# Moving the start addresses of the operands of fp32r products within 256 bytes

## The chip, the cores and the metric

The kernel runs on one core of a Trainium2 chip. The metric is the device time of one execution in microseconds (us), the median of several runs. Before the change it is 2085.33 us (2084.98 to 2087.54, three runs).

## The reference

Two layers (DEPTH 2) over 512 tokens of 1024 features, all in float32. Each layer computes, from a normalised and modulated `h`:

```python
proj = h @ w_in[l]
qa, ka, va, cq, ckv, kr, z, xbc, dt_raw, gates = jnp.split(proj, _IN_OFFSETS, axis=-1)
...  # differential attention oa (4 heads), latent attention ob (8 heads), SSD scan ys (16 heads)
merged = ga * (ya @ w_branch_a[l]) + gb * (yb @ w_branch_b[l]) + gc * (ys @ w_branch_c[l])
x = x + g_m * (merged @ w_out[l])
h = _rmsnorm(x, norm_ffn[l]) * (1 + sc_f) + sh_f
u = _causal_dwconv(h @ ffn_w_up[l], ffn_conv_w[l], ffn_conv_b[l])
ua, uv = jnp.split(u, 2, axis=-1)
x = x + g_f * ((jax.nn.silu(ua) * uv) @ ffn_w_down[l])
```

## The kernel before, in words

Nearly all of TensorE's work is products with model weights. A float32 product is made of three fp32r products: both operands are split into a high part and a rest (`wh`, `wl` for weights, `hh`, `hl` for the normalised activations; `yh`, `yl` for the branch outputs, `mh`, `ml` for the merged ones and `gh`, `gl` for the gated ones), and high times high, high times rest and rest times high are summed in PSUM. `load` (L114) brings 512 KB of weights by DMA from SP's queue into a tile `wr`; `split` (L126) makes `wh` with one ScalarE activation (L132) and `wl` with one VectorE subtraction (L133). Three buffers of each stand in the pool `wp`; they are used in the order 0, 2, 1, 0, 2, 1.

Four forms of product use them:

- `feat_groups` with `mm3` (L140 to L143): the weights are the stationary operand (128 x 128), the activations move, 512 columns at a time. The moving operands are `hh`/`hl`, `yh`/`yl`, `mh`/`ml`, `gh`/`gl`.
- `feat_halves` (L231), around the seams between stages: as before, in two halves of 256 columns. Some of its weights stand in another pool (`wo` beside the out product, `wd` beside the down product) so that they can wait there.
- `tok_groups` (L192, matmuls L220 to L222): the activations `hh`/`hl` are stationary and the weights move, 256 columns at a time. It makes `z` and the queries, keys and values of the differential attention.
- `latent_product` (L269, matmuls L295 to L297): as `tok_groups`, with 432 columns.

While one matmul streams its moving operand, the weights of the next matmul are loaded. A statement about two addresses below is therefore about the moving operand of one matmul and the stationary operand of the next.

The order of TensorE's instructions is written out by hand in the attention stages and at the seams (`manual_schedule`); there the weight products fill the time between the steps of the attention heads. Elsewhere the scheduler of the tile framework orders them. VectorE also sums the modulation vectors (`macc`, L518) in the gaps.

SBUF tiles lie one after another in the order of the pools, 32 bytes the least step. From the tile shapes: the constants (`cst`) begin at byte 16512 of a partition and end at 22720. There `big` begins: `x16` at 22720, `hh` at 39104, `hl` at 55488. `wp` follows at 71872: three `wr`, three `wh` (the first at 84160), three `wl` (96448) of 4096 bytes each, two `wg` of 2048. The small tiles `sm` lie from 112832 to 119936. Above them the stage pools: `gh` begins at 122752, `yh` at 130944, `mh` at 163712. From the top down lie pools of the right side: the first buffer of `wo` begins at 197600, of `wd` at 178112.

Below, the residue of a tile is its start modulo 256, and d is the moving operand's start less the stationary operand's, modulo 256. Tiles are addressed within themselves in steps of 512 bytes or more (except the second 432-column block of a latent tile), so that d is the same along a product. Before the change:

| product | moving | stationary | d |
|---|---|---|---|
| 512 columns, h | 192 | 192 | 0 |
| 512 columns, y, m, g | 128 | 192 | 192 |
| 256 columns, `tok_groups` | 192 (weights) | 192 (h) | 0 |
| 256-column halves of m and g, weights in `wp` or `wd` | 128 | 192 | 192 |
| 256-column halves of m, weights in `wo` | 128 | 224 | 160 |
| 256-column halves of h | 192 | 192 | 0 |
| 432 columns, seven of eight weight groups | 192 (weights) | 192 (h) | 0 |
| 432 columns, last weight group of layer 0 | 128 (weights) | 192 (h) | 192 |

Of the kernel before, what the change touches and what calls it, by code (L numbers as in the profile page):

```python
# [9 lines left out]
F32 = mybir.dt.float32  # L10
F32R = mybir.dt.float32r
I32 = mybir.dt.int32
AF = mybir.ActivationFunctionType
ALU = mybir.AluOpType
# [4 lines left out]
P = 128  # L19
S = 512  # L20
# [45 lines left out]
def trunk_kernel(ctx: ExitStack, tc: tile.TileContext, a: dict, out: bass.AP):  # L66
# [23 lines left out]
    def small(shape, name, bufs=4):  # L90
        return sm.tile(shape, F32, name=name, tag=name, bufs=bufs)
# [5 lines left out]
    nc.vector.memset(ones, 1.0)  # L97
    tri = cst.tile([P, P], F32, name="tri")
    nc.gpsimd.affine_select(tri, ones, pattern=[[1, P]], compare_op=ALU.is_ge, fill=0.0, base=0, channel_multiplier=-1)
    nhalf = cst.tile([P, 1], F32, name="nhalf")  # L100
    nc.vector.memset(nhalf, -0.5)

    sel = cst.tile([P, SSM_H], F32R, name="sel")
    nc.vector.tensor_copy(out=sel, in_=ident[:, 0:SSM_H])
    nc.vector.tensor_copy(out=sel[32:48], in_=ident[0:SSM_H, 0:SSM_H])
    def rstd_of(ss, n, width, name):
        ms = small([P, n], name + "_ms")
        nc.vector.tensor_scalar(out=ms, in0=ss, scalar1=1.0 / width, scalar2=EPS, op0=ALU.mult, op1=ALU.add)
        r = small([P, n], name + "_r")
        nc.gpsimd.tensor_tensor(out=r, in0=ms, in1=nhalf.broadcast_to([P, n]), op=ALU.pow)  # L110
        return r


# [9 lines left out]
            nc.sync.dma_start(out=dst, in_=src)  # L123
        return raw

    def split(raw, n, scales=None, pool=None):  # L126
        hi = (pool or wp).tile([P, 1024], F32R, name="wh")
        lo = (pool or wp).tile([P, 1024], F32R, name="wl")
        for o, m, col in scales or ((0, n, None),):
            sl = slice(o, o + m)  # L130
            if col is None:
                nc.scalar.activation(hi[:, sl], raw[:, sl], AF.Copy)  # L132
                nc.vector.tensor_tensor(out=lo[:, sl], in0=raw[:, sl], in1=hi[:, sl], op=ALU.subtract)  # L133
            else:
                nc.scalar.activation(hi[:, sl], raw[:, sl], AF.Copy, scale=col)
                nc.vector.scalar_tensor_tensor(out=lo[:, sl], in0=raw[:, sl], scalar=col, in1=hi[:, sl],
                                               op0=ALU.mult, op1=ALU.subtract)
        return hi, lo

    def mm3(o, lh, ll, rh, rl, first, last):  # L140
# [51 lines left out]
    def tok_groups(w, segs, hh, hl, evac):  # L192

        width = sum(n for _, n in segs)

        st = {}

        def group(half):
            def prep():
                rows = w[half * 512:(half + 1) * 512, :].rearrange("(k p) c -> p k c", p=P)  # L200
                raw = wp.tile([P, 1024], F32, name="wr", bufs=3)
                rv_, off = raw[:, 0:4 * width].rearrange("p (k c) -> p k c", k=4), 0
                for c, n in segs:
                    nc.sync.dma_start(out=rv_[:, :, off:off + n], in_=rows[:, :, c:c + n])
                    off += n
                return split(raw, 4 * width)

            def mm(weights):
                wh, wl = weights
                if half == 0:  # L210
                    st["banks"] = [mbank().rearrange("p (t c) -> p t c", t=2) for _ in range(2)]
                for t in range(T):
                    bank = st["banks"][t // 2]
                    o = bank[:, t % 2, 0:width]
                    ts_ = slice(t * P, (t + 1) * P)
                    first, last = half == 0 and t % 2 == 0, half == 1 and t % 2 == 1
                    for k in range(4):
                        kk = 4 * half + k
                        sl = slice(k * width, (k + 1) * width)
                        nc.tensor.matmul(o, hh[:, kk, ts_], wh[:, sl], start=first and k == 0, stop=False)  # L220
                        nc.tensor.matmul(o, hh[:, kk, ts_], wl[:, sl], start=False, stop=False)  # L221
                        nc.tensor.matmul(o, hl[:, kk, ts_], wh[:, sl], start=False, stop=last and k == 3)  # L222
                    if last:
                        evac(t // 2, bank)
                    yield 1.28
            return prep, mm
        return [group(0), group(1)]
# [3 lines left out]
    def feat_halves(w, cols, nk, rhs, evac, joint, pool=None, spare=0):  # L231


        st = {}

        def prep():
            out = []
            for k0 in range(0, nk, 4):
                n = min(4, nk - k0)
                raw = load([(0, (n, 256), w[k0 * P:(k0 + n) * P, cols[0]:cols[0] + 256].rearrange("(k p) c -> p k c", p=P))])  # L240
                out.append([x[:, 0:n * 256].rearrange("p (k i c) -> p i k c", k=n, i=2) for x in split(raw, n * 256, None, pool if nk - k0 <= 4 * spare else None)])
            return out

        def mm(weights, h):
            if h == 0 or not joint:
                st["banks"] = [mbank(), mbank()]
            for k in range(nk):
                vh, vl = weights[k // 4]
                xh, xl = rhs(k)
                for i in range(2):  # L250
                    o = st["banks"][i][:, HALF[h]]
                    mm3(o, vh[:, i, k % 4], vl[:, i, k % 4], xh[:, HALF[h]], xl[:, HALF[h]], k == 0, k == nk - 1)
                if k == nk - 1 and not (joint and h == 0):
                    for i in range(2):
                        if joint:
                            evac(i, st["banks"][i])
                        else:
                            evac(i, st["banks"][i][:, HALF[h]], HALF[h])
                yield 0.64
        return prep, mm  # L260
# [8 lines left out]
    def latent_product(l, pool, hh, hl):  # L269
# [4 lines left out]
        def group(g):  # L274
            rows = a["w_in"][l][g * 256:(g + 1) * 256, :].rearrange("(k p) c -> p k c", p=P)
            raw = wp.tile([P, 1024], F32, name="wr", bufs=3)
            rv_ = raw[:, 0:2 * width].rearrange("p (k c) -> p k c", k=2)
            nc.sync.dma_start(out=rv_[:, :, 0:416], in_=rows[:, :, C_CQ:C_CQ + 416])
            nc.sync.dma_start(out=rv_[:, :, 416:width], in_=rows[:, :, C_DT:C_DT + 16])
            return split(raw, 2 * width, None, pool if g == 3 else None)  # L280

        def prep():
            return [group(g) for g in range(3)]
# [94 lines left out]
    def vectors(l, vp):  # L378
# [5 lines left out]
            nc.sync.dma_start(out=t[r:r + n, :], in_=src)  # L384
        rv = rowv[l]
        for nm, key in (("dtb", "ssm_dt_bias"), ("alog", "ssm_a_log"), ("dvec", "ssm_d")):
            t_ = cst.tile([P, SSM_H], F32, name=f"{nm}{l}")
            nc.sync.dma_start(out=t_, in_=a[key][l:l + 1, :].broadcast_to([P, SSM_H]))
            rv[nm] = t_
        rows(r2, 0, a["ssm_conv_b"][l].rearrange("(r p) -> r p", p=P), 16)  # L390
# [30 lines left out]
        lsum = vp.tile([P, 2], F32, name="lsum")  # L421
        nc.vector.tensor_reduce(out=lsum, in_=pr, axis=AX.X, op=ALU.add)
        nc.scalar.activation(lsum, lsum, AF.Exp)
        lam = cst.tile([P, 1], F32, name=f"lam{l}")
        nc.vector.scalar_tensor_tensor(out=lam, in0=lsum[:, 0:1], scalar=0.8 - 0.6 * math.exp(-0.3 * l),
                                       in1=lsum[:, 1:2], op0=ALU.add, op1=ALU.subtract)
        rv["lam"] = lam
        for nm, key in (("q", "mla_q_norm"), ("k", "mla_k_norm")):
            w32 = cst.tile([P, ROPE], F32, name=f"w32{nm}{l}")
            nc.sync.dma_start(out=w32, in_=a[key][l:l + 1, NOPE:MLA_QK].broadcast_to([P, ROPE]))  # L430
            rv["w" + nm] = w32

# [61 lines left out]
    def mod_steps(l, j, pool=None):  # L494
# [27 lines left out]
        def total():  # L522
            mp = mbank()
            for q in range(4):
                ins = nc.tensor.transpose(out=mp[:, q * P:(q + 1) * P], in_=acc[0][:, q * P:(q + 1) * P], identity=ident)
                if pool:
                    tc.keep_in_program_order(ins)
            cs_ = slice(4 * j, 4 * j + 4)
            tot = small([P, 4], "modsum")
            nc.vector.tensor_reduce(out=tot, in_=mp.rearrange("p (q r) -> p q r", q=4), axis=AX.X, op=ALU.add)  # L530
            nc.vector.tensor_tensor(out=mod[l][:, cs_], in0=tot, in1=vec[l][:, cs_], op=ALU.add)

# [171 lines left out]
    def norm_halves(np_, x, l, v_norm, sh0, sc0):  # L704

        s1 = norm_scale(l, v_norm, sc0)
        sacc = np_.tile([P, S], F32, name="sacc")
        hh, hl = h_tiles()
        st = {}

# [31 lines left out]
    def mix(l, x, hh, hl, ckr, cq, latp, scope):  # L742
# [123 lines left out]
        with ssd_scope:  # L866
            tails = []
            for g in range(SSM_G):
# [102 lines left out]
                                            in1=ecs[:, c, hd].unsqueeze(2).broadcast_to([P, 4, SSM_HD]), op=ALU.mult)  # L971
                    nc.vector.tensor_tensor(out=y[:, c], in0=y[:, c], in1=yo, op=ALU.add)
                nc.vector.scalar_tensor_tensor(out=y, in0=y, scalar=0.5, in1=sz, op0=ALU.mult, op1=ALU.mult)
                ss = small([P, T], "yss")
                for c in range(T):
                    jk = sp.tile([P, 256], F32, name="yo", bufs=2)
                    nc.scalar.activation(jk, y[:, c], AF.Square, accum_out=ss[:, c:c + 1])
# [23 lines left out]
        with ExitStack() as att:  # L1001
# [237 lines left out]
            def da_groups(h):  # L1239
                heads[h]["qk"] = qkn = dap.tile([P, T, 256], F32, name="qkn")  # L1240

                def qk_evac(tt, bank):
# [1 line left out]
                    nc.scalar.activation(raw, bank, AF.Copy)  # L1244
                    sq = dap.tile([P, 2, 256], F32, name="sq2", bufs=2)
                    nc.scalar.activation(sq, raw, AF.Square)
                    ss8 = small([P, 8], "dss8")
                    nc.vector.tensor_reduce(out=ss8, in_=sq.rearrange("p t (g d) -> p (t g) d", d=DA_D), axis=AX.X, op=ALU.add)
                    r8 = rstd_of(ss8, 8, 64.0, "dr8")
                    rg = raw.rearrange("p t (g d) -> p (t g) d", d=DA_D)  # L1250
# [30 lines left out]
            def da_unit(h, t):  # L1281
# [32 lines left out]
                def values():  # L1314
# [6 lines left out]
                    if t == T - 1:  # L1321
                        sq = dap.tile([P, T, P], F32, name="sq2", bufs=2)
                        pov = po.rearrange("p (t c) -> p t c", t=T)
                        nc.scalar.activation(sq, pov, AF.Square)
                        ss = small([P, T], "oss")
                        nc.vector.tensor_reduce(out=ss, in_=sq, axis=AX.X, op=ALU.add)
                        r_ = rstd_of(ss, T, 128.0, "on")
                        hd["on"] = dap.tile([P, T, P], F32, name="on", bufs=1)
# [252 lines left out]
```

## Time and profile before

| what | us |
|---|---|
| median of three runs | 2085.33 |
| the profiled execution, its own time | 2087.19 |
| its span, first to last instruction | 2085.2 |
| PE (TensorE matmuls) busy | 2060.7 |
| DVE (VectorE) busy | 1415.1 |
| ACT (ScalarE) busy | 923.4 |

The span is 2 us shorter than the execution's time; the rest lies before the first and after the last instruction. A matmul's record lasts longer than its share of the engine, since matmuls overlap: what one costs in a row of its kind is read from start to start in the timeline, and so done below.

### The profile page before, as it was taken

To read this page: it belongs to the slowest core of one execution; us is meant where nothing else is said; L and a number is where in the kernel's file an instruction comes from. 1 tells how busy PE (TensorE), PEld (TensorE's weight loads), DVE (VectorE), ACT (ScalarE), POOL (GpSimd) and SP (SyncE) were. 2 spreads that over 40 slices of the span, in tenths; PEclk is the share of its full clock that TensorE was granted. 3 is DMA by queue.
4 is the path that set the end of the run, shared out by engine and by line. 5 is a ranking of instruction groups with operands and counts; after the bars stand their busy time and mean duration, and the time that the engine had idled before them with its cause. 6 is when DMAs were issued, how large, how long until landed. Compare 5 with 4: busy or idle time off the path is not lost.

```text
span 2085.2 us, 30158 instructions
## 1 busy us (share of the span) xinstructions
PE 2060.7 (99%) x11469; PEld 1794.4 (86%) x11469; DVE 1415.1 (68%) x2731; ACT 923.4 (44%) x1702; POOL 136.0 (7%) x162
## 2 busy tenths in 40 slices
PE   8999999999999999999999999999999999999999
PEld 7889988899888988888898888889998888888888
DVE  7788887747876778657767887765566566553553
ACT  6744445535533444224344544454444334432431
POOL 4200011002100000000000000110020000000000
PEclk8999999999999999999999999999999999999999
DMA  8523232243455265655443222212333242323322
GB/s 268 154 61 92 71 117 86 86 123 105 143 157 171 85 189 171 193 175 159 156 136 91 71 61 88 64 48 79 95 89 93 91 132 91 101 91 96 97 91 81
DMA packets 224542, 237.20 MB, mean 114 GB/s; under 512 B 16126, under 2 KB 195742, under 8 KB 224142
## 3 DMA queue, kind: packets, MB, share of 16 engines
q1 hardware_dynamic: 221646, 232.63, 36.5%
q0 software_dynamic: 2752, 2.65, 0.5%
q8 instruction: 90, 1.47, 0.3%
q14 instruction: 54, 0.44, 0.1%
HBM read 226.30 MB, written 8.91 MB: 113 GB/s over the span
## 4 chain that ended last, share of the span: by engine, by line
PE 85%; DVE 5%; issue 5%; DMA 2%; POOL 1%; ACT 1%; SPq 0%; POOLq 0%; DVEq 0%; ACTq 0%
PE mb L141 20%; PE mb L142 20%; PE mb L143 20%; PE mb L220 3%; PE mb L222 3%; PE mb L221 3%; PE ab L1168 2%; PE mb L662 1%; PE ab L1136 1%; DMA wg<-in_ada_w_dram 1%; DVE wl L133 1%; PE ab L961 1%; DVE macc L518 1%; PE ab L1319 1%; PE ab L1078 1%
## 5 line engine op out<-in xcount | busy, mean ns | idle before, releaser
L141 PE MATMUL mb<-hh,wh 128*128 128x512 f32 (+1 forms) x1376 | 538.5, 392 | 2.9 <-DVE modsum L530 1.4
L143 PE MATMUL mb<-hh,wl 128*128 128x512 f32 (+1 forms) x1376 | 532.9, 387 | 0.0
L142 PE MATMUL mb<-hl,wh 128*128 128x512 f32 (+1 forms) x1376 | 532.5, 387 | 0.0
L133 DVE TENSOR_TENSOR wl<-wr,wh 128x1024 fp32r<-128x1024 f32 (+2 forms) x312 | 375.2, 1204 | 201.2 <-ACT wh L132 195.5
L132 ACT ACTIVATE wh<-wr 128x1024 fp32r<-128x1024 f32 (+2 forms) x312 | 324.5, 1041 | 337.3 <-PE mb L142 257.4
L141 PEld LDWEIGHTS mb<-hh,wh 128*128 128x128 f32 x1376 | 258.6, 188 | 53.4 <-DVE modsum L530 2.6
L143 PEld LDWEIGHTS mb<-hh,wl 128*128 128x128 f32 x1376 | 258.7, 188 | 51.4
L142 PEld LDWEIGHTS mb<-hl,wh 128*128 128x128 f32 x1376 | 259.0, 188 | 49.0 <-DVE hl L698 1.2
L1416 DVE SCALAR_TENSOR_TENSOR fu<-mb,vec,fu 128x510 f32<-128x510 f32 (+1 forms) x176 | 129.9, 746 | 91.2 <-ACT fu L1414 89.6
L220 PE MATMUL mb<-wh,hh 128*128 128x256 f32 x640 | 182.4, 285 | 0.0
L221 PE MATMUL mb<-wl,hh 128*128 128x256 f32 x640 | 181.2, 283 | 0.0
L222 PE MATMUL mb<-wh,hl 128*128 128x256 f32 x640 | 181.2, 283 | 0.0
L141 PE MATMUL mb<-gh,wh 128*128 128x512 f32 (+1 forms) x432 | 152.3, 353 | 0.0
L143 PE MATMUL mb<-gh,wl 128*128 128x512 f32 (+1 forms) x432 | 151.7, 351 | 0.0
L142 PE MATMUL mb<-gl,wh 128*128 128x512 f32 (+1 forms) x432 | 151.7, 351 | 0.0
L1414 ACT ACTIVATE fu<-mb,vec 128x512 f32<-128x512 f32 x88 | 67.7, 772 | 149.0 <-PE mb L143 149.0
L220 PEld LDWEIGHTS mb<-wh,hh 128*128 128x128 f32 x640 | 122.6, 192 | 0.8 <-ACT wh L132 0.4
L221 PEld LDWEIGHTS mb<-wl,hh 128*128 128x128 f32 x640 | 122.6, 192 | 0.4
L222 PEld LDWEIGHTS mb<-wh,hl 128*128 128x128 f32 x640 | 122.6, 192 | 0.0
L518 DVE SCALAR_TENSOR_TENSOR macc<-wg,c_act,macc 128x512 f32<-128x512 f32 x140 | 104.8, 749 | 22.9 <-DMA wg<-in_ada_w_dram 22.3
L141 PE MATMUL mb<-yh,wh 128*128 128x512 f32 x256 | 105.4, 412 | 0.9 <-ACT g L765 0.9
L142 PE MATMUL mb<-yl,wh 128*128 128x512 f32 x256 | 101.2, 395 | 0.0
(334 smaller groups left out, 3427.4 us busy)
## 6 DMA issues: line engine op xcount, KB each, us to landing
wr<-in_w_in_dram SPq DMA_DIRECT2D x88, 512.0 KB
wr<-in_ffn_w_up_dram SPq DMA_DIRECT2D x88, 512.0 KB
wg<-in_ada_w_dram SPq DMA_DIRECT2D x160, 256.0 KB
wr<-in_ffn_w_down_dram SPq DMA_DIRECT2D x40, 512.0 KB
wr<-in_w_in_dram SPq DMA_DIRECT2D x64, 256.0 KB
wm<-in_ada_w_dram SPq DMA_DIRECT2D x16, 512.0 KB
wr<-in_w_branch_c_dram SPq DMA_DIRECT2D x16, 512.0 KB
wr<-in_w_out_dram SPq DMA_DIRECT2D x16, 512.0 KB
```

Of the source, the lines that this page charges most:

```text
L132: nc.scalar.activation(hi[:, sl], raw[:, sl], AF.Copy)
L133: nc.vector.tensor_tensor(out=lo[:, sl], in0=raw[:, sl], in1=hi[:, sl], op=ALU.subtract)
L141: nc.tensor.matmul(o, lh, rh, start=first, stop=False)
L142: nc.tensor.matmul(o, lh, rl, start=False, stop=False)
L143: nc.tensor.matmul(o, ll, rh, start=False, stop=last)
L220: nc.tensor.matmul(o, hh[:, kk, ts_], wh[:, sl], start=first and k == 0, stop=False)
L221: nc.tensor.matmul(o, hh[:, kk, ts_], wl[:, sl], start=False, stop=False)
L222: nc.tensor.matmul(o, hl[:, kk, ts_], wh[:, sl], start=False, stop=last and k == 3)
L518: ins = nc.vector.scalar_tensor_tensor(out=acc[0], in0=rk, scalar=c_act[:, kk:kk + 1], in1=acc[0], op0=ALU.mult, op1=ALU.add)
L1168: nc.tensor.matmul(po[:, t * P:n], vv[:, j], st["pT"][:, j * P:(j + 1) * P], start=j == 0, stop=j == t)
L1414: nc.scalar.activation(u, bank, AF.Identity, bias=v[:, V_FCB + ti:V_FCB + ti + 1], scale=tap(2))
L1416: nc.vector.scalar_tensor_tensor(out=u[:, s_:], in0=bank[:, 0:S - s_], scalar=tap(2 - s_), in1=u[:, s_:], op0=ALU.mult, op1=ALU.add)
```

## The change

`split` loses its unused scaling argument and gains a shift. In `wp` the tiles `wh` and `wl` become 48 columns (192 bytes) longer, and each use starts at an offset of 0 to 3 times 64 bytes that undoes what the longer tiles add: every `wh` and `wl` then starts at one residue, 64 bytes higher where `shift=1` is passed (`tok_groups`, `feat_halves`, `latent_product`). In another pool the start is that of the tile plus `own`.

The first changed call below is the one in `tok_groups`, the second that in `latent_product`.

```diff
+    LINE = 16
+    uses = [0]
+    def split(raw, n, pool=None, shift=0, own=0):
+        if pool is None:
+            i = -uses[0] % 3
+            uses[0] += 1
+            at = ((i + shift) % 4, (i + 3 + shift) % 4)
+            hi, lo = [wp.tile([P, 1024 + 3 * LINE], F32R, name=nm)[:, LINE * o:LINE * o + n] for nm, o in zip(("wh", "wl"), at)]
+        else:
+            hi, lo = [pool.tile([P, 1024], F32R, name=nm)[:, own:own + n] for nm in ("wh", "wl")]
+        nc.scalar.activation(hi, raw[:, 0:n], AF.Copy)
+        nc.vector.tensor_tensor(out=lo, in0=raw[:, 0:n], in1=hi, op=ALU.subtract)
         return hi, lo
...
-                return split(raw, 4 * width)
+                return split(raw, 4 * width, shift=1)
...
-            return split(raw, 2 * width, None, pool if g == 3 else None)
+            return split(raw, 2 * width, pool if g == 3 else None, 1, 0 if l else LINE)
...
-    nhalf = cst.tile([P, 1], F32, name="nhalf")
+    nhalf = cst.tile([P, 9], F32, name="nhalf")
...
-        ms = small([P, n], name + "_ms")
+        ms = small([P, n], name + "_ms", 2)
...
-        r = small([P, n], name + "_r")
+        r = small([P, n], name + "_r", 3)
...
-            t_ = cst.tile([P, SSM_H], F32, name=f"{nm}{l}")
+            t_ = cst.tile([P, SSM_H], F32, name=nm)
...
-        sacc = np_.tile([P, S], F32, name="sacc")
+        sacc = np_.tile([P, S + 8 * (v_norm == V_NFFN)], F32, name="sacc")
```

The other edits set the sizes of what lies below: the row constants of the two layers (`dtb`, `alog`, `dvec`, `lam`, `w32q`, `w32k`) share one tile each, and small tiles have 2 or 3 buffers where they had 4 (also `modsum` 2, `yss`, `dss8` and `oss` 3). Worked out with these sizes, `cst` ends at 22720 - 480 + 32 = 22272 = 87 x 256, so `x16`, `hh`, `hl` and `wp` start at residue 0; `sm` starts at 113536 and is 832 bytes smaller, so the stage pools start at 119808 = 468 x 256, 128 bytes lower than before, and `yh`, `yl`, `mh`, `ml`, `gh`, `gl` have residue 0. `wo` moves from 224 to 192; `wd` stays at 192. After the change:

| product | moving | stationary | d |
|---|---|---|---|
| 512 columns, h, y, m, g | 0 | 0 | 0 |
| 256 columns, `tok_groups` | 64 (weights) | 0 (h) | 64 |
| 256-column halves of m, g, h, weights in `wp` | 0 | 64 | 192 |
| 256-column halves of m in `wo`, of g in `wd` | 0 | 192 | 64 |
| 432 columns, seven of eight weight groups | 64 (weights) | 0 (h) | 64 |
| 432 columns, last weight group of layer 1 | 192 (weights) | 0 (h) | 192 |

## Rows read from the trace of the kernel before

**Rows 1.** Parts 1 and 4 of the page: busy us by engine; shares of the last chain.

```profile
PE 2060.7 (99%) x11469; PEld 1794.4 (86%) x11469; DVE 1415.1 (68%) x2731; ACT 923.4 (44%) x1702; POOL 136.0 (7%) x162
...
PE 85%; DVE 5%; issue 5%; DMA 2%; POOL 1%; ACT 1%; SPq 0%; POOLq 0%; DVEq 0%; ACTq 0%
```

**Rows 2.** PE by form: line, output<-moving,stationary, shapes, count | busy us, mean ns | idle.

```profile
L141 PE MATMUL mb<-hh,wh 128*128 128x512 f32 x1312 | 520.2, 397 | 2.1 <-DVE modsum L530 1.4 <-DVE g L774 0.7
...
L220 PE MATMUL mb<-wh,hh 128*128 128x256 f32 x640 | 182.4, 285 | 0.0
...
L141 PE MATMUL mb<-gh,wh 128*128 128x512 f32 x272 | 107.6, 396 | 0.0
...
L141 PE MATMUL mb<-yh,wh 128*128 128x512 f32 x256 | 105.4, 412 | 0.9 <-ACT g L765 0.9
...
L1136 PE MATMUL ab<-ident,sb 128*128 128x128 f32 x240 | 42.1, 273 | 0.6 <-DVE mx L1151 0.5
...
L141 PE MATMUL mb<-mh,wh 128*128 128x256 f32 x128 | 36.0, 281 | 0.0
...
L141 PE MATMUL mb<-mh,wh 128*128 128x512 f32 x64 | 25.3, 395 | 0.0
...
L295 PE MATMUL mb<-wh,hh 128*128 128x432 f32 x64 | 23.1, 365 | 1.4 <-ACT wh L132 1.4
...
L141 PE MATMUL mb<-hh,wh 128*128 128x256 f32 x64 | 18.7, 292 | 0.8 <-ACT hh L697 0.8
...
L1467 PE MATMUL ab<-ident,x 128*128 128x128 f32 x32 | 4.2, 276 | 0.3 <-DVE x L1445 0.3
```

**Rows 3.** PE timeline (start us, duration us), h products, 178 starts, first and last.

```profile
1799.70 0.39 PE L143 MATMUL mb<-hh,wl 128*128 128x512 f32 x1
...
1839.83 0.39 PE L143 MATMUL mb<-hh,wl 128*128 128x512 f32 x1
```

**Rows 4.** PE timeline, down products of g, 173 starts, first and last.

```profile
1849.69 0.39 PE L141 MATMUL mb<-gh,wh 128*128 128x512 f32 x1
...
1889.83 0.39 PE L142 MATMUL mb<-gl,wh 128*128 128x512 f32 x1
```

**Rows 5.** PE timeline, token products, 86 starts, first and last.

```profile
245.80 0.28 PE L220 MATMUL mb<-wh,hh 128*128 128x256 f32 x1
...
255.99 0.28 PE L221 MATMUL mb<-wl,hh 128*128 128x256 f32 x1
```

**Rows 6.** PE timeline, halves of m: starts 1, 39 and 63 of one stretch.

```profile
1692.76 0.28 PE L142 MATMUL mb<-ml,wh 128*128 128x256 f32 x1
...
1697.07 0.28 PE L141 MATMUL mb<-mh,wh 128*128 128x256 f32 x1
...
1699.95 0.28 PE L141 MATMUL mb<-mh,wh 128*128 128x256 f32 x1
```

**Rows 7.** PE timeline, halves of g after a restart, 79 starts, first and last.

```profile
1072.80 0.28 PE L141 MATMUL mb<-gh,wh 128*128 128x256 f32 x1
...
1081.99 0.28 PE L141 MATMUL mb<-gh,wh 128*128 128x256 f32 x1
```

**Rows 8.** PE timeline, y products in an attention stage, 36 starts, first and last.

```profile
617.82 0.40 PE L142 MATMUL mb<-yl,wh 128*128 128x512 f32 x1
...
625.99 0.40 PE L141 MATMUL mb<-yh,wh 128*128 128x512 f32 x1
```

**Rows 9.** PE timeline, h products just after SSD matmuls, 37 starts, first and last.

```profile
188.69 0.39 PE L141 MATMUL mb<-hh,wh 128*128 128x512 f32 x1
...
196.89 0.39 PE L141 MATMUL mb<-hh,wh 128*128 128x512 f32 x1
```

**Rows 10.** Windows: stretch, busy us (count) of each engine, PEclk, DMA share, GB/s.

```profile
552.00:640.00 88.00, 86.36 (x425) 71.47 (x424) 67.53 (x128) 36.60 (x67) 5.60 (x6) 1.00 0.52 162
```

**Rows 11.** The last chain (start us, us): the head of the latent attention, layer 0.

```profile
293.20 1.02 POOL r_r L110
...
297.84 0.09 DVE r_ms L108
```

More of the change, by code (lines that the diff above doesn't have):

```diff
@@ L106, in rstd_of @@
     def rstd_of(ss, n, width, name):
-        ms = small([P, n], name + "_ms")
+        ms = small([P, n], name + "_ms", 2)
         nc.vector.tensor_scalar(out=ms, in0=ss, scalar1=1.0 / width, scalar2=EPS, op0=ALU.mult, op1=ALU.add)
-        r = small([P, n], name + "_r")
-        nc.gpsimd.tensor_tensor(out=r, in0=ms, in1=nhalf.broadcast_to([P, n]), op=ALU.pow)
+        r = small([P, n], name + "_r", 3)
+        nc.gpsimd.tensor_tensor(out=r, in0=ms, in1=nhalf[:, 0:1].broadcast_to([P, n]), op=ALU.pow)
         return r
@@ L124, in load @@
         return raw
[L126 to L137, printed above, removed]
+    LINE = 16
[10 more added lines that the diff above has]
+        nc.vector.tensor_tensor(out=lo, in0=raw[:, 0:n], in1=hi, op=ALU.subtract)
         return hi, lo
@@ L240, in prep @@
                 raw = load([(0, (n, 256), w[k0 * P:(k0 + n) * P, cols[0]:cols[0] + 256].rearrange("(k p) c -> p k c", p=P))])
-                out.append([x[:, 0:n * 256].rearrange("p (k i c) -> p i k c", k=n, i=2) for x in split(raw, n * 256, None, pool if nk - k0 <= 4 * spare else None)])
+                out.append([x[:, 0:n * 256].rearrange("p (k i c) -> p i k c", k=n, i=2) for x in split(raw, n * 256, pool if nk - k0 <= 4 * spare else None, 1)])
             return out
@@ L423, in vectors @@
         nc.scalar.activation(lsum, lsum, AF.Exp)
-        lam = cst.tile([P, 1], F32, name=f"lam{l}")
+        lam = cst.tile([P, 1], F32, name="lam")
         nc.vector.scalar_tensor_tensor(out=lam, in0=lsum[:, 0:1], scalar=0.8 - 0.6 * math.exp(-0.3 * l),
@@ L428, in vectors @@
         for nm, key in (("q", "mla_q_norm"), ("k", "mla_k_norm")):
-            w32 = cst.tile([P, ROPE], F32, name=f"w32{nm}{l}")
+            w32 = cst.tile([P, ROPE], F32, name=f"w32{nm}")
             nc.sync.dma_start(out=w32, in_=a[key][l:l + 1, NOPE:MLA_QK].broadcast_to([P, ROPE]))
@@ L528, in total @@
             cs_ = slice(4 * j, 4 * j + 4)
-            tot = small([P, 4], "modsum")
+            tot = small([P, 4], "modsum", 2)
             nc.vector.tensor_reduce(out=tot, in_=mp.rearrange("p (q r) -> p q r", q=4), axis=AX.X, op=ALU.add)
@@ L973, in mix @@
                 nc.vector.scalar_tensor_tensor(out=y, in0=y, scalar=0.5, in1=sz, op0=ALU.mult, op1=ALU.mult)
-                ss = small([P, T], "yss")
+                ss = small([P, T], "yss", 3)
                 for c in range(T):
@@ L1246, in qk_evac @@
                     nc.scalar.activation(sq, raw, AF.Square)
-                    ss8 = small([P, 8], "dss8")
+                    ss8 = small([P, 8], "dss8", 3)
                     nc.vector.tensor_reduce(out=ss8, in_=sq.rearrange("p t (g d) -> p (t g) d", d=DA_D), axis=AX.X, op=ALU.add)
@@ L1324, in values @@
                         nc.scalar.activation(sq, pov, AF.Square)
-                        ss = small([P, T], "oss")
+                        ss = small([P, T], "oss", 3)
                         nc.vector.tensor_reduce(out=ss, in_=sq, axis=AX.X, op=ALU.add)
```

## The prediction

> **What bounds the kernel now.** I read the page's busy times first, then the shares of the last chain: TensorE is busy for 2060.7 of 2085.2 us and makes 85% of the chain [rows 1]. So the kernel ends when TensorE has issued its matmuls, and a nanosecond off each of them shortens it. A matmul's own duration does not show this price, because matmuls overlap (390 ns recorded, another start every 230 ns); the timeline does, from start to start. The forms by count [rows 2] say how many there are of each; each row stands for one of three product lines, so the counts below are its count times three.
>
> From start to start, two products of the same shape cost different times:
>
> - 512 columns, h: 1839.83 - 1799.70 = 40.13 us over 177 steps, 226.7 ns [rows 3].
> - 512 columns, g: 40.14 us over 172 steps, 233.4 ns [rows 4]; y in an attention stage: 8.17 us over 35 steps, 233.4 ns [rows 8].
> - 256 columns, token products: 10.19 us over 85 steps, 119.9 ns [rows 5].
> - 256 columns, halves of m: 4.31 us over 38 steps, 113.4 ns; then, from the first matmul whose weights come from the pool `wo`, 2.88 us over 24 steps, 120.0 ns [rows 6]. Nothing else changes at that point: moving tile, columns and engine order stay.
>
> The last pair is the best evidence that the address matters: with the weights at residue 192 (d 192) it is 113.4, at 224 (d 160) 120.0. Set beside the table of residues the rows read: at 512 columns d 0 costs 226.7 and d 192 costs 233.4; at 256 columns d 0 and d 160 cost 120 and d 192 costs 113.4. One thing disturbs this: after a restart, halves of g at d 192 ran at 9.19 us / 78 = 117.8 ns [rows 7].
>
> **The change, part by part.** It removes and adds no matmul, no split and no load; it moves addresses.
>
> *512 columns, g and m.* 3 x (272 + 64) = 1008 matmuls [rows 2] go from d 192 to d 0, so from 233.4 to 226.7 if the h rows hold for them [rows 3, 4]: 1008 x 6.7 = 6.8 us. They stand in long runs. Bounds: nothing, and 6.8 us.
>
> *512 columns, y.* 3 x 256 = 768 [rows 2], in short runs between attention steps. Products of h that follow a break take 8.20 us / 36 = 227.8 ns [rows 9], and shorter runs will do worse; so at most 768 x 5.6 = 4.3 us, at least nothing. I take 3.2, three quarters, because most y runs are shorter than that stretch.
>
> *512 columns, h.* 3 x 1312 = 3936 matmuls keep d 0 but all move from residue 192 to 0. I cost that at nothing: what differs between rows so far is explained by d. If the place itself mattered, the bound is 3936 x 6.7 = 26.4 us lost (the slowest 512-column row [rows 4] for all of them); a gain has no row, 226.7 being the fastest of that width.
>
> *256 columns, token products.* 3 x 640 = 1920 [rows 2] go from d 0 to d 64, the largest term and the least certain, since no product in the trace has d 64. The weights end up 64 bytes above the activations in both forms, but here the weights move, so that d is +64, where the 113.4 rows have 192, which is -64. The nearest rows bound it: at 113.4 [rows 6] the gain is 1920 x 6.5 = 12.5 us; at 117.8 [rows 7] it is 4.0; at 120.0 [rows 6] nothing. A loss beyond that has no row at 256 columns. I take 11.5: the step off d 0 is as large as in the fast rows, and I know no reason for a sign, with 1 us off for the short runs of the differential attention that begin after a break.
>
> *Halves and 432 columns.* The 192 h halves [rows 2] go from d 0 to d 192: 1.2 us at most, 0.4 at the 117.8 of rows 7; I take 0.8. The 96 m halves with weights in `wo` go from d 160 to 64: by the token argument 96 x 6.6 = 0.6, or nothing. The 120 g halves with weights in `wd` go from 192 to 64: nothing, or 0.8 us lost. The 3 x 64 matmuls of 432 columns [rows 2] gain or lose at most the 256-column difference, 1.2 us; I take nothing. Together 1.4.
>
> *Transposes.* The identity keeps its place while what it turns moves by 128 bytes. Records with d 0 last 273 ns, with the identity 64 bytes below `x` (d 192) 276 ns [rows 2], nearly none; I take nothing, and 3 ns on each of these 272, 0.8 us, as the bound either way.
>
> *Smaller buffers.* A `ms` tile is now used again two calls on, so VectorE's tensor_scalar (L108) may wait for the GpSimd power of two calls before, with the splits and `macc` sums of VectorE's queue behind it and TensorE's weights behind those. In the densest place, the head of the latent attention, the power of the first call starts at 293.20 and takes 1.02 us; the third call writes its `ms` at 297.84 [rows 11], 3.6 us after that power ended. I cost it at nothing; the cover gone, one call costs up to 1.02 us. Row constants shared between layers make their loads on SP's queue, and the weight loads behind them, wait for readers in layer 0's attention and SSD; those loads stand behind layer 0's seam in program order, long after. Nothing.
>
> *The sum.* 6.8 + 3.2 + 11.5 + 1.4 = 22.9 us of TensorE's time. Not all reaches the end: in the stretch around the second half of the differential attention TensorE is busy 86.36 of 88 us and VectorE 67.53 [rows 10], and over the span it idles 24.5 us [rows 1]; where VectorE, ScalarE or GpSimd is late already, faster filling makes TensorE wait longer. I take 1.4 off: 21.5. The profiled execution took 2087.19 us, so 2065.7 on its own scale; it lies 1.86 above the median of three, which gives 2063.8 for a median. I forecast 2064.
>
> **A rule against it.** In the profile two products equal in columns, engine and clock differ by 6.6 ns when only the stationary tile's place changes [rows 6]. The Trainium skill (TensorE: Matmul & The Clock Gate, step-by-step in "Part 2: What happens when you issue a matmul") says that loading the next weights doesn't steal SBUF read bandwidth from the running matmul, and the section "Who interferes with whom" of SBUF — State Buffer that "PE and ACT never wait on anyone". By that rule no address could matter; the trace disagrees where it can be read, and the rule survives only if `wo` differs from `wp` in something else. Its section "Back-to-back issue gap" gives N / 2.4 + 2.5 ns, 215.8 at 512 columns; the 226.7 of rows 3 is 11 above it.
>
> **The rivals.**
>
> 1. *d 64 is not d 192.* If the token products stay at 120, the `wo` term falls away and the `wd` halves lose 0.8: 6.8 + 3.2 + 0.8 - 0.8 = 10.0, less 0.6 on the way, 9.4: 2076. For it: no row has d 64, and 160 is no better than 0, so not every distance from 0 helps. Against: nothing in the trace either.
> 2. *d 64 settles at the pace of rows 7*, 117.8: 4.0 in place of 11.5, and about 0.5 less for the rest: 13.6: 2072. For it: breaks before runs bring that pace on in the trace. Against: other halves of the same kind returned to 113.4.
> 3. *Not the address.* The g, y and m products differ from h in their tiles and stages, not only in d; if the 226.7 belongs to h for another reason, and the 120.0 to `wo` for being another pool, nothing moves: 2085. Against: the switch within one stretch in rows 6. This is the time that the two pages above would give.
> 4. *The place itself counts, not d: slower.* All 512-column products with 226.7 have their moving operand at 192, all with 233.4 at 128; moving residue and d cannot be told apart in these rows. If residue 192 is what is fast and 0 is like 128, the 3936 h products go to 233.4: 26.4 us lost, with nothing won on y, m and g. Even with the whole token and halves gain of 13 us the kernel is slower, about 2099; without it 2112. It decides once half of the h products fall back, and it shows in the first layer's SSD products. Against: d explains the 256-column rows, where `wo` changes only the stationary side.
>
> **How the numbers follow.** The forecast, 0.46; rival 1, 0.20; rival 2, 0.12; rival 3, 0.10; rival 4, 0.10; waits from the smaller buffers that eat half of a gain, 0.02. The likeliest has its own range of 2061 to 2068. For 8 in 10 I reach over rivals 1 and 2, with about 1 us for the transposes at the lower side and 3 above for smaller token gains: 2060 to 2080. A difference under 0.2% (4 us) can't be told from none. Faster: 0.46 + 0.20 + 0.12 + 0.01 = 0.79; the same: rival 3 and half of the buffer case, 0.11; slower: rival 4, 0.10.
>
> **What would show it.** Start to start in the profile after: g, m and y at 226 to 229 ns (right) or 233 (wrong); h still at 226.7, where 233 is rival 4; token products at 113 to 114 (forecast), 118 (rival 2) or 120 (rival 1). TensorE's busy time should fall by about as much as the span. The prediction is wrong if the span falls by less than 5 us, or if it falls by 20 while these rates stand: then the gain came from the order of the work, not from addresses.

## The result and the profile after

The kernel after takes 2076.13 us in the median of five runs (2075.1 to 2078.33), beside 2087.54 for the kernel before (five runs): a ratio of 0.9947, 95% interval 0.9936 to 0.9957. That is 11.4 us or 0.53% less, about half of the 21.5 us forecast; the measured time lies inside the stated range. (This median of before is 2.2 us above the one that the forecast started from.)

The page of the kernel after, its span and busy times, answering to [rows 1]:

```profile
span 2074.4 us, 30171 instructions
...
PE 2047.5 (99%) x11469; PEld 1790.2 (86%) x11469; DVE 1414.3 (68%) x2731; ACT 924.0 (45%) x1702; POOL 135.6 (7%) x162
```

TensorE issues the same 11469 matmuls and is busy 13.2 us less; the span is 10.8 us shorter, so TensorE idles 26.9 us where it idled 24.5. It is still the bound. In the code after, the product lines stand four lower: `mm3` is L145 to L147, the token products are L224 to L226.

Next, TensorE's timeline of the kernel after (start us, duration us, line, operation, tiles): pairs of one long run each, in the order h, g, m at 512 columns, y in the attention stage, then a token run of the SSD scan. The price is the time from the first row to the last over the steps between them.

```profile
1759.62 0.39 PE L147 MATMUL mb<-hh,wl 128*128 128x512 f32 x1
...
1799.97 0.39 PE L145 MATMUL mb<-hh,wh 128*128 128x512 f32 x1
...
1859.81 0.39 PE L145 MATMUL mb<-gh,wh 128*128 128x512 f32 x1
...
1898.79 0.39 PE L146 MATMUL mb<-gl,wh 128*128 128x512 f32 x1
...
663.74 0.39 PE L146 MATMUL mb<-ml,wh 128*128 128x512 f32 x1
...
682.33 0.39 PE L147 MATMUL mb<-mh,wl 128*128 128x512 f32 x1
...
617.05 0.39 PE L146 MATMUL mb<-yl,wh 128*128 128x512 f32 x1
...
627.53 0.39 PE L147 MATMUL mb<-yh,wl 128*128 128x512 f32 x1
...
202.68 0.28 PE L224 MATMUL mb<-wh,hh 128*128 128x256 f32 x1
...
213.75 0.28 PE L225 MATMUL mb<-wl,hh 128*128 128x256 f32 x1
```

- h: 40.35 us over 178 steps, 226.7 ns, as in [rows 3], though its tiles went from residue 192 to 0. The place itself does not count at 512 columns.
- g: 38.98 us / 172 = 226.6; m: 18.59 / 82 = 226.7; y: 10.48 / 46 = 227.8. Before, g and y stood at 233.4 [rows 4, 8] and m at 233.3 in the same view. They moved from d 192 to d 0.
- Token products, d 0 to 64: 11.07 us / 94 = 117.8, not the 113.4 that was taken; 119.9 before [rows 5].

The halves of g at the seam show the two paces of 256 columns in one run. Same view of the kernel after; the first two rows lie in its first part, the last two in its end:

```profile
1048.92 0.28 PE L145 MATMUL mb<-gh,wh 128*128 128x256 f32 x1
...
1062.70 0.28 PE L145 MATMUL mb<-gh,wh 128*128 128x256 f32 x1
...
1062.94 0.28 PE L147 MATMUL mb<-gh,wl 128*128 128x256 f32 x1
...
1065.66 0.28 PE L147 MATMUL mb<-gh,wl 128*128 128x256 f32 x1
```

13.78 us / 117 = 117.8, then 2.72 / 24 = 113.3. In the kernel before, this run is at 113.3 from start to end. Its weights in `wp` kept d 192, so the distance alone doesn't set the pace of a 256-column product. At 1062.9 the weights change from `wd` (d 64) back to `wp` (d 192). In layer 1, where all weights of these halves stand in `wp`, the run at the same place keeps 117.8 to its end. The granted clock is 1.00 in the windows of both paces (the upper of its two levels, 2.4 GHz), so the clock does not tell them apart.

Where the span's time went, in windows cut at the same matmul in both kernels (columns: window, length, then the busy time and count of PE, PEld, DVE, ACT, POOL, then the granted clock, DMA share and GB/s). Of before: the start up to the first token run in two windows, the stretch with the first SSD scan, the seam of layer 0 with its halves of g, the end.

```profile
0.00:69.63 69.63, 59.46 (x323) 55.20 (x323) 56.31 (x177) 51.86 (x116) 33.14 (x55) 0.90 0.72 234
69.63:113.46 43.83, 42.38 (x207) 37.19 (x205) 33.26 (x85) 23.78 (x57) 2.36 (x2) 1.00 0.51 147
113.46:451.35 337.89, 334.71 (x2073) 299.38 (x2073) 260.38 (x563) 164.95 (x355) 28.14 (x26) 1.00 0.30 88
...
1053.85:1102.08 48.23, 48.23 (x354) 47.47 (x353) 34.10 (x70) 23.23 (x54) 1.39 (x2) 1.00 0.47 142
...
2049.51:2085.20 35.69, 31.33 (x273) 30.73 (x271) 10.57 (x20) 6.45 (x10) 0.00 (x0) 1.00 0.23 82
```

The same five of after:

```profile
0.00:70.29 70.29, 59.39 (x322) 55.23 (x323) 56.53 (x177) 52.08 (x116) 32.91 (x55) 0.90 0.72 232
70.29:114.58 44.29, 42.68 (x207) 37.13 (x205) 33.25 (x85) 23.91 (x57) 2.36 (x2) 1.00 0.50 142
114.58:451.37 336.79, 333.11 (x2074) 298.10 (x2073) 260.26 (x563) 164.92 (x355) 28.14 (x26) 1.00 0.31 89
...
1048.92:1097.52 48.60, 48.60 (x354) 47.93 (x353) 34.19 (x70) 23.22 (x54) 1.39 (x2) 1.00 0.45 141
...
2037.97:2074.40 36.43, 32.08 (x273) 31.48 (x271) 10.55 (x20) 6.45 (x10) 0.00 (x0) 1.00 0.23 80
```

Up to the first token run 1.1 us are lost, 0.9 of it idle time (in the profiles of the kernels below the first token run starts between 112.7 and 118.0, so this part varies). The end, halves of g and the closing transposes, is 0.7 us longer with TensorE 0.75 us busier, and the seam of layer 0, where halves of g stand too, is 0.4 us longer. The other windows gain.

### The profile page after: what moved, and what is told of

Same layout as the page of the kernel before. It is cut to its first block, busy times and chain, and to the rows that moved or that the text cites. A ratio compares the mean times of both kernels' runs of the same rounds, so it can differ in the third digit from the quotient of the medians.

```text
span 2074.4 us, 30171 instructions
## 1 busy us (share of the span) xinstructions
PE 2047.5 (99%) x11469; PEld 1790.2 (86%) x11469; DVE 1414.3 (68%) x2731; ACT 924.0 (45%) x1702; POOL 135.6 (7%) x162
## 4 chain that ended last, share of the span: by engine, by line
PE 88%; DVE 6%; DMA 3%; issue 1%; POOL 1%; ACT 1%; SPq 0%; DVEq 0%; POOLq 0%; ACTq 0%
PE mb L145 21%; PE mb L147 21%; PE mb L146 21%; PE mb L224 3%; PE mb L226 3%; PE mb L225 3%; PE ab L1172 2%; PE ab L965 1%; PE ab L1140 1%; DMA wg<-in_ada_w_dram 1%; DVE wl L141 1%; DVE macc L522 1%; PE mb L666 1%; PE ab L1082 1%; PE ab L1323 1%
## 5 line engine op out<-in xcount | busy, mean ns | idle before, releaser
L145 PE MATMUL mb<-hh,wh 128*128 128x512 f32 (+1 forms) x1376 | 538.6, 392 | 2.6 <-DVE g L778 1.0
L147 PE MATMUL mb<-hh,wl 128*128 128x512 f32 (+1 forms) x1376 | 532.6, 387 | 0.0
L145 PEld LDWEIGHTS mb<-hh,wh 128*128 128x128 f32 x1376 | 258.4, 188 | 52.8 <-DVE modsum L534 1.9
L147 PEld LDWEIGHTS mb<-hh,wl 128*128 128x128 f32 x1376 | 258.5, 188 | 51.6
L224 PE MATMUL mb<-wh,hh 128*128 128x256 f32 x640 | 180.2, 282 | 0.0
L226 PE MATMUL mb<-wh,hl 128*128 128x256 f32 x640 | 178.7, 279 | 0.0
L145 PE MATMUL mb<-gh,wh 128*128 128x512 f32 (+1 forms) x432 | 151.3, 350 | 0.0
L147 PE MATMUL mb<-gh,wl 128*128 128x512 f32 (+1 forms) x432 | 150.7, 349 | 0.0
L224 PEld LDWEIGHTS mb<-wh,hh 128*128 128x128 f32 x640 | 120.2, 188 | 0.8 <-ACT wh L140 0.4
L226 PEld LDWEIGHTS mb<-wh,hl 128*128 128x128 f32 x640 | 120.2, 188 | 0.0
L145 PE MATMUL mb<-yh,wh 128*128 128x512 f32 x256 | 104.4, 408 | 1.2 <-ACT g L769 1.2
L147 PE MATMUL mb<-yh,wl 128*128 128x512 f32 x256 | 100.4, 392 | 0.0
```

What stands on the lines that cost most here:

```text
L145: nc.tensor.matmul(o, lh, rh, start=first, stop=False)
L147: nc.tensor.matmul(o, ll, rh, start=False, stop=last)
```

## The experiments

Paces below are means over all clean steps of a kind, from the start times of the trace to the nanosecond; a step is clean if it is under 130 ns at 256 columns, 215 at 432 and 260 at 512, so that waits fall out. Each was timed in five rounds against the kernel before, whose median was 2087.3 to 2088.1 us in these jobs.

**Only the 512-column part.** The shift is taken back from the 256- and 432-column products:

```diff
-                return split(raw, 4 * width, shift=1)
+                return split(raw, 4 * width)
```

and likewise in `feat_halves` and `latent_product`.

> The changed kernel with the 64-byte shift taken back: token products, halves in wp and latent products at d 0, the 512-column products still all at d 0. Theory A (each form's gain is its start-to-start gain times its count): token products back at 119.9 ns, halves in wp at 120; 1920 x 2.4 = 4.6 us and about 600 halves x 2.5 = 1.5 us more than the changed kernel, so some 6 us slower than it, 5.5 us faster than before. Rival (only the order of the work moved): the same time as the changed kernel within 2 us.

2083.29 us, ratio 0.9978 [0.9969, 0.9987]. One token run of its timeline:

```profile
206.50 0.28 PE L224 MATMUL mb<-wh,hh 128*128 128x256 f32 x1
...
216.93 0.28 PE L224 MATMUL mb<-wh,hh 128*128 128x256 f32 x1
```

10.43 us / 87 = 119.9, as before; 512 columns as after. Halves of h stand at 119.5; those of g and m, in part still at d 64 with their weights in `wd` and `wo`, at 118.2 each. So at d 0 the 256-column products have the old pace, and the shift is what took the token products to 117.4. Against after, the rates give 1920 x 2.5 = 4.8 us for the token products, 1.0 for the halves of h and 1.5 for those of m and g, 7.3 together; the medians differ by 7.2 (2083.29 - 2076.13).

**Token products at d 192** instead of 64:

```diff
-                return split(raw, 4 * width, shift=1)
+                return split(raw, 4 * width, shift=3)
```

> The changed kernel with the moving weights of the token products at residue 192 in place of 64, so d 192 as in the halves. Theory A (one row of distance: two paces, 113.3 and 117.8, are open to any d of 64 or 192, and what stands before the run picks one): token products stay at 117.8 in most runs, the time stays within 2 us of the changed kernel. Theory B (the sign of d is what was mis-sized): token products at 113.4, 1920 x 4.1 = 7.9 us faster than the changed kernel, about 2068 us.

2072.54 us, ratio 0.9929 [0.9917, 0.9942]; mean pace 115.7. That mean is of two: a run behind small matmuls (first pair) and one directly behind h products (second pair).

```profile
114.83 0.28 PE L226 MATMUL mb<-wh,hl 128*128 128x256 f32 x1
...
123.90 0.28 PE L225 MATMUL mb<-wl,hh 128*128 128x256 f32 x1
...
245.76 0.28 PE L226 MATMUL mb<-wh,hl 128*128 128x256 f32 x1
...
255.89 0.28 PE L225 MATMUL mb<-wl,hh 128*128 128x256 f32 x1
```

9.07 / 80 = 113.4 and 10.13 / 86 = 117.8. So d 64 is worse than d 192 in the mean: the forecast's step from one to the other does not hold. But d 192 does not give 113.4 by itself either; the outcome lies between both theories.

**Token products at d 128** (`shift=2` in the same line).

> The changed kernel with the moving weights of the token products at residue 128: d 128. Theory A says only that 64 and 192 have the two paces. If two residues off is as good as one: 113.3 or 117.8, the time between 2068 and 2077 us. If d 128 is like d 0: 120 ns, 4.6 us slower than the changed kernel.

2079.05 us, ratio 0.9959 [0.9947, 0.9972]; mean pace 118.9. At 256 columns d 128 lies between d 0 (120) and d 64 (117.4), and it has two paces of its own, 118.7 and 120.0 (the table below).

**The last 512-column products put at d 192**, ahead of the token runs and the halves. `feat_groups` gets an argument `lead`, 1 where a 256-column run follows:

```diff
-                wh, wl = split(raw, n * 256)
+                wh, wl = split(raw, n * 256, shift=lead if k0 + n == nk else 0)
```

> The changed kernel with the last weight group (24 matmuls) of the 512-column products that stand ahead of the SSD token products (8 places) and ahead of the halves of m and g (3 places) at d 192 again. Theory A (a run of 256-column products takes over a pace from the matmuls before it): these 264 matmuls at 233.3 cost 264 x 6.7 = 1.8 us, and the 768 token products behind them fall from 117.8 to 113.3 (3.4 us), the first stretches of halves (some 400) too (1.8 us): 3 us faster than the changed kernel. Rival (the pace belongs to d or to the tiles): 117.8 stays, 1.8 us slower.

2079.68 us, ratio 0.9963 [0.9951, 0.9976]. The 264 led matmuls went to 233, and the 256-column runs kept their paces (token 117.4, halves of g 116.9, of m 115.9). That they inherit 113.3 from products at d 192 falls in this form.

**Everything 128 bytes higher at the same distances:**

```diff
-    nhalf = cst.tile([P, 9], F32, name="nhalf")
+    nhalf = cst.tile([P, 41], F32, name="nhalf")
```

> The kernel after with everything from `big` on the left side 128 bytes higher: distances stay as they are (512 columns 0, token products 64), but the tiles that stood at residues 0 and 64 stand at 128 and 192; the halves whose weights lie in `wo` and `wd`, on the right side, go from d 64 to d 192 by it. Theory (only the distance counts, and at d 64 and 192 what came before a run): every pace as in the kernel after at its distance, 512 columns 226.7 and token products 117.4 ns; only the 216 halves with `wo` and `wd` weights may go from 117.8 to 113.4: 2075 to 2077 us. Rival (the place counts in 256-column products): halves at residues 128 and 192, the place they had before the change, run at 113.4 from their first matmul, and the token products move too: 480 x 3.5 ns = 1.7 us less for the halves, 2074, and up to 1920 x 4.1 ns = 7.9 us less if the token products go to 113.3: 2066.

2075.16 us, ratio 0.9943 [0.9929, 0.9958]. Its halves of g, now at residues 128 and 192 as before the change and at d 192 to the end:

```profile
1048.72 0.28 PE L145 MATMUL mb<-gh,wh 128*128 128x256 f32 x1
...
1064.86 0.28 PE L147 MATMUL mb<-gh,wl 128*128 128x256 f32 x1
```

16.14 / 137 = 117.8 throughout. The place does not bring 113.3 back, and without a change of distance at `wd` the run does not change its pace. Token products: 116.9, the six SSD runs behind h products at 117.8 as in after.

**Both: 128 bytes higher, token products at d 192.**

> As e5_place, with the token products at d 192 as in e2_tok_192, so that all 256-column products stand at d 192. Theory (distance and history): as e2_tok_192, token products 115.7 ns in the mean with runs at 113.3 and at 117.8, 2072 to 2073 us. Rival (the place counts): all of them at 113.3, 1920 x 2.4 ns = 4.6 us and 1.7 us for the halves less: 2066 us.

2074.33 us, ratio 0.9936 [0.9921, 0.9952]; token products 115.5, halves of g 116.9. The theory's paces, and its 2072 to 2073 lies within the interval; the rival's 2066 is outside the interval (0.9921 x 2088.1 = 2071.6).

**A break ahead of the SSD token runs**, on top of e2_tok_192:

```diff
+                brk = abank()
+                for c in range(4):
+                    nc.tensor.transpose(out=brk[:, c * P:(c + 1) * P], in_=ident, identity=ident)
                 lin_tok(w_in, [(C_Z + 256 * g, 256)], hh, hl, ev_z)
```

> As e2_tok_192, with four transposes of the identity, into a bank that nobody reads, between the 512-column products and the token run of z in the SSD stages, eight places; at two of them other small matmuls stood there already. Theory (a token run at d 192 that begins after a break with other matmuls takes the pace of 113.3, one that follows 512-column products directly that of 117.8): the six runs go from 117.8 to 113.3, 6 x 96 x 4.5 ns = 2.6 us less, against 8 x 4 transposes at 0.06 to 0.11 us, 1.8 to 3.5 us more: 2072 to 2074 us, and the pace in those runs tells. Rival (what stands before does not set the pace): the six runs stay at 117.8, 2074 to 2076 us.

2076.88 us, ratio 0.9949 [0.9934, 0.9964]. Two of its runs behind the same four transposes:

```profile
157.34 0.60 PE L909 MATMUL ab<-ident 128*128 128x128 f32 x4
...
158.82 0.28 PE L224 MATMUL mb<-wh,hh 128*128 128x256 f32 x1
...
168.57 0.28 PE L226 MATMUL mb<-wh,hl 128*128 128x256 f32 x1
...
244.13 0.60 PE L909 MATMUL ab<-ident 128*128 128x128 f32 x4
...
245.16 0.28 PE L226 MATMUL mb<-wh,hl 128*128 128x256 f32 x1
...
254.93 0.28 PE L225 MATMUL mb<-wl,hh 128*128 128x256 f32 x1
```

9.75 / 86 = 113.4 and 9.77 / 83 = 117.7. Four of the six runs went to 113.3, two did not, and the two that had been at 113.3 behind other small matmuls went to 117.8. A break makes either pace possible; it does not choose one. The theory falls as a rule, and the median lies above both forecasts.

**512 columns at d 64** (`shift=3` for every weight group of `feat_groups`).

> The kernel after with the weights of the 512-column products 64 bytes lower than the activations (d 64 instead of 0); all else as after. Theory (at 512 columns any distance but 0 costs as d 192 does): 233.3 in place of 226.7 ns, 5712 x 6.6 ns = 37.7 us more: 2113 us. Rival (the sign of the distance counts at 512 columns): 226.7 or less stays, 2076 us, or something between; the pace from start to start tells.

2084.22 us, ratio 0.9983 [0.9972, 0.9994]. Its h products, then its halves of g, which keep d 192:

```profile
1779.77 0.39 PE L147 MATMUL mb<-hh,wl 128*128 128x512 f32 x1
...
1819.83 0.39 PE L145 MATMUL mb<-hh,wh 128*128 128x512 f32 x1
...
1051.28 0.28 PE L145 MATMUL mb<-gh,wh 128*128 128x256 f32 x1
...
1065.90 0.28 PE L145 MATMUL mb<-gh,wh 128*128 128x256 f32 x1
```

40.06 / 175 = 228.9: not the theory's 233.3, but the "something between" that the rival allowed. And 14.62 / 129 = 113.3 for halves whose own addresses are those of after, where they ran at 117.8: what stands ahead of a run sets its pace.

**The last 512-column group at d 64** (e4's edit with `shift=3 * lead`), token products at d 192.

> As e2_tok_192 (token products at d 192), with the last weight group (24 matmuls) of the 512-column products that stand directly ahead of the SSD token runs and of the halves put at d 64, 264 matmuls in eleven places. Theory (a 256-column run at d 192 keeps the pace at which it locks to the matmuls before it; behind 512-column products at d 64 that is 113.3, as the halves of e8_512_d64 show, behind those at d 0 it is 117.8): the six SSD token runs that stand directly behind h products go from 117.8 to 113.3, 6 x 96 x 4.5 ns = 2.6 us, the four runs of halves likewise, some 460 x 3.5 ns = 1.6 us, less 264 x 2.3 ns = 0.6 us for the led products: 3.6 us below e2_tok_192, 2069. Rival (what counts is not the distance just before, as in e4_lead, where a last group at d 192 changed no pace): the 256-column runs keep their paces, 2073.

2072.57 us, ratio 0.9924 [0.9912, 0.9937]. Four of the six SSD token runs went to 113.3; the other two and all halves stayed. The two kinds of start, the last 512-column row and the first of 256:

```profile
1163.38 0.39 PE L147 MATMUL mb<-hh,wl 128*128 128x512 f32 x1
1163.61 0.28 PE L224 MATMUL mb<-wh,hh 128*128 128x256 f32 x1
...
1173.97 0.28 PE L225 MATMUL mb<-wl,hh 128*128 128x256 f32 x1
...
1206.75 0.40 PE L147 MATMUL mb<-hh,wl 128*128 128x512 f32 x1
1206.99 0.28 PE L224 MATMUL mb<-wh,hh 128*128 128x256 f32 x1
...
1216.98 0.28 PE L225 MATMUL mb<-wl,hh 128*128 128x256 f32 x1
```

The first starts 0.23 us behind (227 ns in the trace) and takes 10.36 us for 88 steps, 117.7 ns each; the second starts 0.24 behind (236 ns) and takes 9.99 for 88, 113.5, its first steps being longer. Set against all the kernels above, this step from the last 512-column matmul to the first of 256 columns sorts the runs at d 192, and gave a rule to test: 232 ns or more, and the run takes 113.3.

**512 columns at d 128.**

> The kernel after with the weights of the 512-column products 128 bytes from the activations (d 128); all else as after. Theory (the cost grows with the distance upward from 0 to 192: 226.7 at 0, 229.0 at 64, 233.3 at 192): about 231, 5712 x 4.4 ns = 25 us more than after if all of it reached the end; in e8_512_d64 8 of 10 us did, so about 2097. Rival (128 is a place of its own, as with token products, where 128 gave 118.9 between 117.4 and 120): 226.7 or 233.3, 2076 or 2112.

2099.57 us, ratio 1.0063 [1.0049, 1.0077], slower than before.

```profile
1779.76 0.39 PE L146 MATMUL mb<-hl,wh 128*128 128x512 f32 x1
...
1819.96 0.39 PE L145 MATMUL mb<-hh,wh 128*128 128x512 f32 x1
```

40.20 / 173 = 232.4. The price at 512 columns grows from d 0 over 64 and 128 to 192: 226.7, 228.9, 232.4 and 233.3, the order that the theory expected.

**The rule tested: the last h group at d 192** (e4's edit ahead of the SSD token runs only), token products at d 192.

> As e2_tok_192 (token products at d 192), with the last weight group (24 matmuls) of the 512-column h products ahead of the eight SSD token runs at d 192, 192 matmuls; the halves are left as in after. Theory (what settles the pace of a run at d 192 is how late its first matmul starts behind the last 512-column one: in the kernels so far the runs with 232 ns or more went to 113.3, those with 231 or less to 117.8; in e4_lead the same led products came 233 to 236 before the token runs): all six SSD token runs behind h products go to 113.3, 6 x 96 x 4.5 ns = 2.6 us, less 192 x 6 ns = 1.2 us for the led products: 1.4 us below e2_tok_192, 2071. Rival (that rule is chance, or belongs to other products than these): some or all of the six stay at 117.8, up to 1.2 us above e2_tok_192: 2073 to 2074.

2072.34 us, ratio 0.993 [0.9918, 0.9942]. One run of each kind:

```profile
158.28 0.39 PE L147 MATMUL mb<-hh,wl 128*128 128x512 f32 x1
158.51 0.28 PE L224 MATMUL mb<-wh,hh 128*128 128x256 f32 x1
...
169.46 0.28 PE L224 MATMUL mb<-wh,hh 128*128 128x256 f32 x1
...
1205.54 0.40 PE L147 MATMUL mb<-hh,wl 128*128 128x512 f32 x1
1205.78 0.28 PE L224 MATMUL mb<-wh,hh 128*128 128x256 f32 x1
...
1216.45 0.28 PE L225 MATMUL mb<-wl,hh 128*128 128x256 f32 x1
```

10.95 us / 93 = 117.7 and 10.67 / 94 = 113.5. Windows over these two runs:

```profile
158.51:169.46 10.95, 10.95 (x94) 10.95 (x93) 8.57 (x11) 4.71 (x7) 0.00 (x0) 1.00 0.52 139
1205.78:1216.45 10.67, 10.67 (x96) 10.67 (x94) 8.62 (x12) 4.76 (x7) 0.00 (x0) 1.00 0.51 133
```

Granted clock and DMA share are the same in both, 1.00 and 0.52 or 0.51, so neither makes the difference. Five of the six started 233 to 236 ns behind and settled at 113.3; the one that started 228 behind stayed at 117.8. So the rule held in all six, though the edit did not make all six late. The gain over e2_tok_192 can't be told from none in the medians; mean pace of the token products 114.6 against 115.7.

Over the thirteen kernels, all runs of 23 or more 256-column products directly behind 512-column ones, by the step into the run (pace once settled; d is that of the run's first weights):

| d of the run | step into it, ns | runs | pace, ns |
|---|---|---|---|
| 192 | 223 to 231 | 72 | 117.8 |
| 192 | 232 to 236 | 20 | 113.3 |
| 64 | 224 to 225 | 4 | 113.3 |
| 64 | 226 to 240 | 46 | 117.8 |
| 0 | 224 to 236 | 24 | 120 |
| 128 | 227 | 4 | 120.0 |
| 128 | 224, 225, 231 to 233 | 6 | 118.7 |

The limit at d 192 was tested by e11_lead_192 alone; the one at d 64, and d 128, are read from these same runs. Token runs directly behind 256-column matmuls of the attention (`ab<-kl,qk`), again 23 or more, show the same two orders: at d 64 all 21 with a step of 113 to 118 ns took 113.3 and all 26 with 120 to 122 took 117.8; at d 192 all 12 with 113 or 114 took 117.8 and 19 of 20 with 120 took 113.3. Between these (119 at d 64, 116 to 119 at d 192) both paces come.

The three kernels with token products at d 192 and the tiles in the places of after (e2, e9, e11) take 2072.3 to 2072.6 us, some 3.6 below the kernel after, though their intervals still touch its own. They can't be told apart from each other.

## Why the prediction was half right

The terms, each pace of the profiled pair times its count:

| term | forecast, us | measured, us |
|---|---|---|
| 512 columns, g and m | 6.8 | 816 x 6.48 + 192 x 6.67 = 6.6 |
| 512 columns, y | 3.2 | 768 x 4.54 = 3.5 |
| 512 columns, h | 0 | 3936 x -0.05 = -0.2 |
| token products | 11.5 | 1920 x 2.4 = 4.6 |
| halves and 432 columns | 1.4 | 1.0 (h) - 1.3 (g) - 0.1 (m) + 0.1 (432) = -0.3 |
| sum | 22.9 | 14.2 |
| not at the end | -1.4 | -3.4 |
| span | 21.5 | 10.8 |

**The step that failed** is the token term: "I take 11.5: the step off d 0 is as large as in the fast rows, and I know no reason for a sign". There is a sign. At 256 columns, d 64 and d 192 each have two paces, 113.3 and 117.8, and which one a run takes is settled as it begins. Behind the h products at d 0, with steps of 226 to 233 ns into the run, a run at d 64 takes 117.8 (the table above), and so do most of the other token runs of the kernel after; in the mean the 1920 products gained 2.4 ns each. This is rival 2, and its term was 4.0. It had a row: [rows 7] showed 117.8 at a distance whose other rows read 113.4, and I put it down to a restart and gave it 0.12.

**The halves** missed for the same reason. The g halves in `wp` kept their distance and their cost was put at nothing; but the products ahead of them went from d 192 to d 0, the step into the run shortened to 225 or 226 ns, and they fell from 113.3 to 117.8, in layer 0 until the weights changed pool, in layer 1 for the whole run of 144. A change to one product cost the next one. E8_512_d64 shows it the other way round.

**Right:** the 512-column terms, in mechanism and size; that h would not move, and so that rival 4 (the place) is wrong, shown by h after and by e5_place; that the smaller buffers cost nothing (VectorE's L108 waits for no GpSimd power in the trace after). Rival 3, not the address, falls with e8 and e10, which change only weight addresses and cost 8 and 23 us. Rival 1's price for d 64, 120, is not what was measured; that its total, 2076, is the measured time is luck: it took nothing for the token products, where 4.6 were measured, it lost 0.6 on the way, where 3.4 were, and it started from a median of before that was 2.2 lower.

The rule weighed against the change, that loading the next weights takes no read bandwidth from the running matmul (the Trainium skill, TensorE: Matmul & The Clock Gate, "Part 2: What happens when you issue a matmul"), from which the prediction took that no address could matter, has no place for the four prices of one 512-column product that differ by address alone. That page's formula for an isolated matmul, N / 2.4 + 2.5 ns in "Back-to-back issue gap", gives 109.2 at 256 columns, an estimate; the best steady pace at that width in any run here is 113.3.

**On the way** 3.4 us were lost, not 1.4. TensorE idles 2.4 us longer: 0.9 up to the first token run, which varies between kernels, 0.5 in the stretch with the first SSD scan, 0.6 between 451 and 663 us (1.6 before, 2.2 after) and 0.4 from 1622 us to the last halves (0.6 before, 1.0 after). The other 1.0 is the difference between the sum of rates (14.2) and the fall of TensorE's busy time (13.2). No single wait carries it.

**Open:** why the step into a run goes with its pace, and what settles a run whose step lies between the two groups. That the weights' distance and what stands ahead of a run together set its pace is shown (e2_tok_192 and e8_512_d64); the step sorts the runs and foretold those of e11_lead_192, but no run changes it with all addresses kept, so it may be a sign of the cause and not the cause. What in the engine or in SBUF does it is not shown. The residues are worked out from the tile shapes; no view prints an address.

## What to carry to other kernels

Read the price of a product from start to start, at each residue distance between the moving operand and the next stationary one, and give the widest and most frequent products the cheapest distance; the price at one distance does not carry over to its mirror image (d 192 to d 64 here). Where the same product shows two paces in one trace, look at what stands directly ahead of each run before multiplying either by a count. A faster product can cost the next one its pace, so count the neighbours of what is moved too.

## What the runs showed that I had not expected

- A 256-column run keeps one of two paces, 113.3 or 117.8 ns, over 94 and more matmuls, and a difference of a few ns in its first step (231 or 232 at d 192, 225 or 226 at d 64) goes with the one or the other.
- At 512 columns, of the runs of 60 matmuls and more, all 20 of the kernel after (d 0) settled at 226.7 and all 8 at d 192 in before at 233.3. At d 64, 19 of 20 settled at 228.9 and one at 233.3; at d 128, 12 at 232.4 and 8 at 233.3. So a second pace is not peculiar to 256 columns, and of the two cheapest distances d 0 alone had a single pace.
